# Forming the lower weight halves of some feed-forward units by an adding DMA

## The chip, the cores and the metric

One core of a Trainium2 chip runs the whole program. The metric is the time of one execution on the device in microseconds (us), the median over runs. Beside it stands the profile of one execution, taken by the hardware profiler: for each instruction its engine, its line in the kernel, its start and length, and what it waited for. TensorE appears as PE (matmuls) and PEld (loads of its stationary operand), VectorE as DVE, ScalarE as ACT, GpSimd as POOL, and SyncE, which issues most DMAs, as SP.

## What is computed

Two layers of an encoder trunk on a sequence of 256 positions with 1024 channels, in float32:

```python
for l in range(DEPTH):                       # DEPTH = 2
    h = swiglu(rmsnorm(x, ffn1_pre_g[l]), ffn1_w_in[l], ffn1_w_out[l])
    x = x + 0.5 * rmsnorm(h, ffn1_post_g[l])
    h = hybrid_mixer(rmsnorm(x, mix_pre_g[l]), ...)   # LRU, retention, short convolution
    x = x + rmsnorm(h, mix_post_g[l])
    h = swiglu(rmsnorm(x, ffn2_pre_g[l]), ffn2_w_in[l], ffn2_w_out[l])
    x = x + 0.5 * rmsnorm(h, ffn2_post_g[l])

def swiglu(u, w_in, w_out):                  # w_in 1024 x 5632, w_out 2816 x 1024
    gate, up = split(u @ w_in, 2)
    return (silu(gate) * up) @ w_out
```

There are four feed-forward stages (two in each layer) and two mixers. The change touches the feed-forward stages alone.

## The kernel before

**Weights as a stream of units.** All large weight matrices lie in HBM in the order in which they are used, cut into 568 units of 128 rows by 1024 columns (512 KB). Two neighbouring units make a pair, 1 MB, loaded by one DMA from SP's queue into a buffer named raw (line 88; three such buffers). TensorE multiplies in a reduced form of float32 (fp32r), so each unit is split in two: ACT rounds it to an upper part, tile whi (line 93), and DVE subtracts that from the raw weights to give a lower part, tile wlo (line 94). The activations are split likewise, and each product is three matmuls into the same accumulator (`mm3`, lines 272 to 275): upper activations by whi (L273), upper activations by wlo (L274), lower activations by whi (L275).

**How far the stream runs ahead.** There are eight buffers for whi and eight for wlo. `Stream.prep` forms the next unit. `Stream.fill` forms units until eight are alive, and `Stream.done` drops units that are used up and calls `fill`. A unit's buffer is that of the unit eight places before it, so its whi can be written only when TensorE has read the older one for the last time.

**A feed-forward stage** (`ffn`, line 307) has eleven steps s = 0 to 10, each of 256 hidden channels. A step takes four units of the input projection, `ui[s]`, and two of the output projection, `uo[s]`. In the stream they stand as ui[0], ui[1], uo[0], ui[2], uo[1], ui[3] and so on. In the middle of a stage (lines 365 to 375) one step runs like this on TensorE: `fin(s, 0)` and `fin(s, 1)` multiply the two blocks of 128 positions by the four units ui[s], 24 matmuls each; then `fout(s-1, 0)`, two transpositions of step s (`ftr`, line 334), `fout(s-1, 1)`, and two more transpositions. Each unit of ui[s] serves six matmuls in a row of a `fin`. ACT and DVE form silu(gate) times up (lines 325 and 326) behind each `fin`, and they split the transposed result (lines 258 and 259) behind each `ftr`.

**Order of the work.** The program's text gives each instruction a priority. A planner then lays the instructions on the engines, taking by priority what its own model of the machine holds ready, and each engine keeps that order on the chip. On each engine and each queue instructions start in order: one that waits holds back what stands behind it on the same engine.

**POOL in a feed-forward stage.** At the ends of stages POOL does two small operations of each normalisation (lines 201 and 202). In the first feed-forward stage it also computes constants of the mixer once, a chain of 24 small operations (`channel_consts`, lines 448 to 471, called through `mixer_consts` at step 4 in the text). Otherwise it does nothing there, and it issues no DMA anywhere in the kernel.

Of the kernel before, what the change touches and what calls it, by code (L numbers as in the profile page):

```python
# [11 lines left out]
F32 = mybir.dt.float32  # L12
# [3 lines left out]
ALU = mybir.AluOpType  # L16
# [12 lines left out]
UW = 1024  # L29
# [41 lines left out]
class Stream:  # L71


    def __init__(self, nc, wpool, w):
        self.nc, self.pool, self.w = nc, wpool, w
        self.n = 2 * w.shape[0]
        self.next = 0
        self.tiles = {}
        self.cur = 0

    def prep(self):
        nc, i = self.nc, self.next
        n = UW // 2 if i < FIRST else UW
        if i % 2 == 0:
            self.raw = self.pool.tile([P, 2 * UW], F32, tag="raw", name=f"raw{i}", bufs=RBUFS)
            m = n if i < FIRST else 2 * UW
            for k in range(0, 2 * UW, m):
                nc.sync.dma_start(self.raw[:, k:k + m], self.w[i // 2, :, k:k + m])
        raw = self.raw[:, (i % 2) * UW:(i % 2 + 1) * UW]
        hi = self.pool.tile([P, UW], F32R, tag="whi", name=f"whi{i}", bufs=WBUFS)  # L90
        lo = self.pool.tile([P, UW], F32R, tag="wlo", name=f"wlo{i}", bufs=WBUFS)
        for k in range(0, UW, n):
            nc.scalar.copy(hi[:, k:k + n], raw[:, k:k + n])  # L93
            nc.vector.tensor_sub(lo[:, k:k + n], raw[:, k:k + n], hi[:, k:k + n].bitcast(F32))  # L94
        self.tiles[i] = (hi, lo)
        self.next += 1

# [22 lines left out]
def trunk_kernel(ctx: ExitStack, tc: tile.TileContext, x_in, pos, gains, gain0, par, id_in, consts, gw, w, out):  # L120
    nc = tc.nc
# [16 lines left out]
    def tok():  # L138
        return tp.tile([P, 512], F32, tag="tok", name=nm("tok"), bufs=TOK)
# [4 lines left out]
    def spl(shape):  # L144
        return tp.tile(shape, F32R, tag="spl", name=nm("spl"), bufs=7)
# [7 lines left out]
    def ps_tr():  # L153
        return pp.tile([P, 512], F32, tag="tr", name=nm("pstr"), bufs=2)

    def ps_acc():
        return [pp.tile([P, 512], F32, tag="acc", name=nm("psacc"), bufs=4) for _ in range(2)]
# [31 lines left out]
    st = Stream(nc, wp, w)  # L189
# [66 lines left out]
    def split(h, lo, src, scale=None):  # L256
        if scale is None:
            act.copy(h, src)  # L258
            dve.tensor_sub(lo, src, h.bitcast(F32))  # L259
        else:  # L260
            act.mul(h, src, scale)
            dve.scalar_tensor_tensor(lo, src, scale, h.bitcast(F32), op0=ALU.mult, op1=ALU.subtract)

    def post(tb, acc, l, k, f, fast=False):
        r = rstd(acc, D, f, fast)
        t = halves(w4())
        for o, a, g in zip(t, acc, halves(gain_tiles[(l, k)])):
            dve.tensor_mul(o, a, g)
        for a, o in zip(t, halves(x[tb])):
            dve.scalar_tensor_tensor(o, a, r, o, op0=ALU.mult, op1=ALU.add)  # L270
# [6 lines left out]
    def inproj(us, tb, turn=None):  # L277

        ps = ps_in()
        for c in range(KD):  # L280
            if c == KD - 3 and turn is not None:
                turn()
            h, lo = st.get(us[c // 2])
            s = slice((c % 2) * 512, (c % 2 + 1) * 512)
            mm3(ps, uh[tb][:, c, :], ul[tb][:, c, :], h[:, s], lo[:, s], c == 0, c == KD - 1)
        return ps

    def inproj2(us):

        ps = [ps_in() for _ in range(NTB)]  # L290
        for k, u in enumerate(us):
            h, lo = st.get(u)
            for tb in range(NTB):
                for i in range(2):
                    c, s = 2 * k + i, slice(i * 512, (i + 1) * 512)
                    mm3(ps[tb], uh[tb][:, c, :], ul[tb][:, c, :], h[:, s], lo[:, s], c == 0, c == KD - 1)
        return ps

    def outproj(acc, blocks, us, first, last, ns=(0, 1)):

        for n in ns:
            for i, ((ah, al), u) in enumerate(zip(blocks, us)):
                h, lo = [halves(t)[n] for t in st.get(u)]
                mm3(acc[n], ah, al, h, lo, first and i == 0, last and i == len(us) - 1)


    def ffn(l, kpost, after, turn, during=None, start=False, fast=False):


        ui, uo, hT = {}, {}, {}  # L310
        for s in range(NS + 1):
            if s < NS:
                ui[s] = st.take(4)
            if s >= 1:
                uo[s - 1] = st.take(2)
        acc = [ps_acc() for _ in range(NTB)]

        def fin(s, tb, turn=None):
            gate_up(s, tb, [inproj(ui[s], tb, turn)])

        def gate_up(s, tb0, pss):
            for tb, ps in enumerate(pss, tb0):
                t = tok()
                with tc.high_priority(offset=CHAIN_LEAD if s == NS - 1 else 0):
                    act.activation(t[:, 0:256], ps[:, 0:256], AF.Silu, scale=fac[tb])  # L325
                    dve.scalar_tensor_tensor(t[:, 256:512], ps[:, 256:512], fac[tb], t[:, 0:256],  # L326
                                             op0=ALU.mult, op1=ALU.mult)
                hT[(s, tb)] = t

        def ftr(s, tb):  # L330
            t = hT[(s, tb)]
            pt = ps_tr()
            for i in range(2):
                pe.transpose(pt[:, i * P:(i + 1) * P], t[:, 256 + i * P:256 + (i + 1) * P], ident)  # L334
            hl = spl([P, 2, 256])
            with tc.high_priority(offset=CHAIN_LEAD if s == NS - 1 else 0):
                split(hl[:, 0, :], hl[:, 1, :], pt[:, 0:256])
            hT[(s, tb)] = hl

        def fout(s, tb, ns=(0, 1)):  # L340
            hl = hT[(s, tb)]
            outproj(acc[tb], [(hl[:, 0, c * P:(c + 1) * P], hl[:, 1, c * P:(c + 1) * P]) for c in range(2)],
                    uo[s], s == 0, s == NS - 1, ns)

        st.fill()
        if start:
            gate_up(0, 0, inproj2(ui[0]))
            st.done(ui[0])
            fin(1, 0)
            ftr(0, 0)  # L350
        else:
            fin(0, 0)
            fin(1, 0, turn)
            ftr(0, 0)
            fin(0, 1)
            st.done(ui[0])
        ftr(1, 0)
        fin(1, 1)
        ftr(0, 1)
        st.done(ui[1])  # L360
        fout(0, 0)
        fout(0, 1)
        ftr(1, 1)
        st.done(uo[0])
        for s in range(2, NS - 1):
            if s == 4 and during is not None:
                during()
            fin(s, 0)
            fin(s, 1)
            st.done(ui[s])  # L370
            fout(s - 1, 0)
            ftr(s, 0)
            fout(s - 1, 1)
            ftr(s, 1)
            st.done(uo[s - 1])
        e = NS - 1

        def tail(tb):
            fin(e, tb)
            fout(e - 1, tb, (0,))  # L380
            ftr(e, tb)
            fout(e - 1, tb, (1,))

        tail(0)
        fout(e, 0)
        with tc.high_priority(offset=CHAIN_LEAD):
            post(0, acc[0], l, kpost, 0.5)
            turn = after(0)
        tail(1)
        st.done(ui[e])  # L390
        st.done(uo[e - 1])
        fout(e, 1, (0,))
        if turn is not None:
            turn()
        fout(e, 1, (1,))
        st.done(uo[e])
        with tc.high_priority(offset=CHAIN_LEAD):
            post(1, acc[1], l, kpost, 0.5, fast)
            return after(1)
# [492 lines left out]
    for l in range(L):  # L892
        turn = ffn(l, G_F1POST, lambda tb: pre(tb, l, G_MPRE, False), turn,
                   mixer_consts if l == 0 else lambda: load_gain(l, G_MPRE), l == 0)
        load_gain(l, G_MPOST)
        load_gain(l, G_F2PRE)
        turn = mixer(l, lambda tb: pre(tb, l, G_F2PRE, True), turn)
        load_gain(l, G_F2POST)
        if l + 1 < L:
            load_gain(l + 1, G_F1PRE)  # L900
            turn = ffn(l, G_F2POST, lambda tb: pre(tb, l + 1, G_F1PRE, True), turn)
            load_gain(l + 1, G_F1POST)
        else:
            ffn(l, G_F2POST, store, turn, fast=True)
# [120 lines left out]
```

## Time and profile before

| | |
|---|---|
| median of 3 runs | 1677.73 us (1677.65 to 1677.97) |
| the profiled execution, its own time | 1678.78 us |
| its span, from the first to the last instruction | 1677.0 us |
| mean granted clock of TensorE | 0.997 of full speed |
| TensorE matmul busy | 1663.1 us (99% of the span) |
| DVE busy | 1069.0 us (64%) |
| ACT busy | 862.0 us (51%) |
| POOL busy | 78.6 us (5%) |
| read from HBM | 307.52 MB, 184 GB/s over the span |

Busy shares are averages over the whole span. Matmul records overlap their neighbours, so the length of one record is not its share of the time; the distance between the starts of two is. Idle time of an engine other than the one that sets the end costs nothing by itself. The launch and the end of a run lie outside the span: 1.78 us in the profiled execution.

### The profile page before, as it was taken

Reading aid. Unit: us, or ns where it says so; the run is one execution under the profiler, and the core shown is the slowest. Engines: PE = TensorE matmul, PEld = TensorE weight load, DVE = VectorE, ACT = ScalarE, POOL = GpSimd, SP = SyncE. Lnnn points to the kernel's source line nnn. Section 1 sums busy time; section 2 is a strip of 40 time slices with the busy share of each in tenths; the row PEclk is TensorE's granted clock in tenths of the full one; section 3 lists DMA queues with packets and bytes.
Section 4 is the critical chain, followed back from the end, with each engine's and each line's share of the span. In section 5 each row is a group of like instructions: output and inputs, shape, how many; then the busy total and the mean of one; then the engine's idle time right before and its main releaser. Section 6 shows DMA issues by size and latency. Waiting matters only on the chain.

```text
span 1677.0 us, 19458 instructions
## 1 busy us (share of the span) xinstructions
PE 1663.1 (99%) x7649; PEld 1372.3 (82%) x7649; DVE 1069.0 (64%) x1329; ACT 862.0 (51%) x1191; POOL 78.6 (5%) x110
## 2 busy tenths in 40 slices
PE   8999999999999999999999999999999999999998
PEld 7888788888888888888888887888888888888886
DVE  6655669956665657655565556799666566675553
ACT  6444567644544445544454445766445545464442
POOL 0300100000000002000000001000000000020000
PEclk9999999999999999999999999999999999999999
DMA  7555454555454444554465554545554454455451
GB/s 300 222 185 191 166 199 163 201 200 199 153 193 158 176 176 176 202 199 176 154 247 192 185 186 165 203 173 201 188 191 174 157 194 152 176 186 201 177 200 50
DMA packets 45163, 309.83 MB, mean 185 GB/s; under 512 B 5136, under 2 KB 5520, under 8 KB 8848
## 3 DMA queue, kind: packets, MB, share of 16 engines
q1 hardware_dynamic: 42768, 301.18, 49.2%
q10 hardware_dynamic: 2304, 7.41, 1.3%
q8 instruction: 60, 0.98, 0.2%
q14 instruction: 31, 0.25, 0.0%
HBM read 307.52 MB, written 1.05 MB: 184 GB/s over the span
## 4 chain that ended last, share of the span: by engine, by line
PE 97%; DVE 1%; issue 1%; POOL 0%; DMA 0%; ACT 0%; DVEq 0%; POOLq 0%; ACTq 0%
PE psin L273 21%; PE psin L274 21%; PE psin L275 21%; PE psacc L275 9%; PE psacc L273 9%; PE psacc L274 9%; PE pstr L334 1%; PE pstr L513 1%; DVE wlo L94 1%; PE pstr L237 1%; PE pstr L678 1%; PE pstr L750 0%; DMA g<-in_gain_dram 0%; PE pstr L274 0%; PE pstr L273 0%
## 5 line engine op out<-in xcount | busy, mean ns | idle before, releaser
L94 DVE TENSOR_TENSOR wlo<-raw,whi 128x1024 fp32r<-128x1024 f32 (+1 forms) x570 | 687.3, 1218 | 365.2 <-ACT whi L93 345.2
L93 ACT CAST whi<-raw 128x1024 fp32r<-128x1024 f32 (+1 forms) x570 | 591.6, 1049 | 295.0 <-PE psacc L275 148.3
L273 PE MATMUL psin<-whi,uh 128*128 128x512 f32 x1600 | 632.3, 395 | 2.8 <-ACT whi L93 2.3
L274 PE MATMUL psin<-wlo,uh 128*128 128x512 f32 x1600 | 626.1, 391 | 0.0
L275 PE MATMUL psin<-whi,ul 128*128 128x512 f32 x1600 | 624.7, 391 | 0.0
L273 PEld LDWEIGHTS psin<-whi,uh 128*128 128x128 f32 x1600 | 301.2, 188 | 62.9 <-ACT whi L93 2.5
L275 PEld LDWEIGHTS psin<-whi,ul 128*128 128x128 f32 x1600 | 300.9, 188 | 62.6
L274 PEld LDWEIGHTS psin<-wlo,uh 128*128 128x128 f32 x1600 | 301.2, 188 | 59.9 <-DVE wlo L94 0.6
L273 PE MATMUL psacc<-whi,spl 128*128 128x512 f32 x608 | 241.3, 397 | 0.0
L275 PE MATMUL psacc<-whi,spl 128*128 128x512 f32 x608 | 237.9, 391 | 0.7 <-DVE spl L259 0.7
L274 PE MATMUL psacc<-wlo,spl 128*128 128x512 f32 x608 | 237.2, 390 | 0.0
L275 PEld LDWEIGHTS psacc<-whi,spl 128*128 128x128 f32 x608 | 114.1, 188 | 25.5 <-DVE spl L259 1.5
L274 PEld LDWEIGHTS psacc<-wlo,spl 128*128 128x128 f32 x608 | 114.4, 188 | 22.2
L273 PEld LDWEIGHTS psacc<-whi,spl 128*128 128x128 f32 x608 | 114.2, 188 | 21.8
L325 ACT ACTIVATE tok<-psin,small 128x256 f32<-128x256 f32 x88 | 41.8, 475 | 173.2 <-PE psin L275 172.0
L326 DVE SCALAR_TENSOR_TENSOR tok<-psin,small,tok 128x256 f32<-128x256 f32 x88 | 42.3, 480 | 113.8 <-ACT tok L325 113.7
L201 POOL TENSOR_SCALAR small<-small 128x1 f32<-128x1 f32 x39 | 39.6, 1015 | 1545.0 <-ACT w L196 1544.3
L258 ACT CAST spl<-pstr 128x256 fp32r<-128x256 f32 (+1 forms) x104 | 41.1, 403 | 56.2 <-PE pstr L334 56.0
L259 DVE TENSOR_TENSOR spl<-pstr,spl 128x256 fp32r<-128x256 f32 (+1 forms) x104 | 47.3, 461 | 26.0 <-ACT spl L258 26.0
L501 ACT COPY tok<-psin 128x512 f32<-128x512 f32 x40 | 23.5, 587 | 62.7 <-PE psin L275 62.7
L258 ACT CAST spl<-w 128x1024 fp32r<-128x1024 f32 x16 | 16.6, 1051 | 40.7 <-DVE w L691 38.9
L334 PEld LDWEIGHTS pstr<-ident,tok 128*128 128x128 f32 x176 | 24.1, 139 | 15.1 <-DVE tok L326 4.0
(146 smaller groups left out, 957.6 us busy)
## 6 DMA issues: line engine op xcount, KB each, us to landing
raw<-in_w_dram SPq DMA_DIRECT2D x283, 1024.0 KB, 4.8
gain<-in_gains_dram ACTq DMA_DIRECT2D x10, 512.0 KB, 4.4
w<-in_gw_dram ACTq DMA_DIRECT2D x4, 512.0 KB, 3.5
x<-in_x_dram SPq DMA_DIRECT2D x2, 512.0 KB, 4.9
raw<-in_w_dram SPq DMA_DIRECT2D x4, 256.0 KB, 6.0
out_dram<-x SPq DMA_DIRECT2D x4, 256.0 KB, 2.0
ks<-in_consts_dram SPq DMA_DIRECT2D x1, 512.5 KB, 5.8
gain<-in_gains_dram SPq DMA_DIRECT2D x1, 512.0 KB, 5.7
```

The source lines that it names most:

```text
L93: nc.scalar.copy(hi[:, k:k + n], raw[:, k:k + n])
L94: nc.vector.tensor_sub(lo[:, k:k + n], raw[:, k:k + n], hi[:, k:k + n].bitcast(F32))
L201: first_e.tensor_scalar(r, ss[:, 0:1], more, EPS / (f * f), op0=ALU.add, op1=ALU.add)
L258: act.copy(h, src)
L259: dve.tensor_sub(lo, src, h.bitcast(F32))
L273: pe.matmul(ps, lhsT=xh, rhs=wh, start=first, stop=False)
L274: pe.matmul(ps, lhsT=xh, rhs=wl, start=False, stop=False)
L275: pe.matmul(ps, lhsT=xl, rhs=wh, start=False, stop=last)
L325: act.activation(t[:, 0:256], ps[:, 0:256], AF.Silu, scale=fac[tb])
L326: dve.scalar_tensor_tensor(t[:, 256:512], ps[:, 256:512], fac[tb], t[:, 0:256], op0=ALU.mult, op1=ALU.mult)
L334: pe.transpose(pt[:, i * P:(i + 1) * P], t[:, 256 + i * P:256 + (i + 1) * P], ident)
L501: act.copy(t, ps)
```

## The change

In each feed-forward stage the numbers of the second and fourth unit of every `ui[s]` are put into a set, in the first stage from s = 2 on. When `prep` comes to a unit of the set, it no longer subtracts on DVE. Instead ACT writes the raw weights times -1 into wlo, which rounds them to fp32r as the upper part was, so wlo holds the negated upper part. Then a DMA issued by POOL reads the same unit of the weights from HBM a second time and adds it onto wlo in place. The result is again the weights less their upper part. All other units keep the subtraction.

```diff
@@ class Stream
+        self.summed = set()
@@ prep
             nc.scalar.copy(hi[:, k:k + n], raw[:, k:k + n])
-            nc.vector.tensor_sub(lo[:, k:k + n], raw[:, k:k + n], hi[:, k:k + n].bitcast(F32))
+            if i in self.summed:
+
+                nc.scalar.mul(lo, raw, -1.0)
+                nc.gpsimd.dma_start(lo, self.w[i // 2, :, (i % 2) * UW:(i % 2 + 1) * UW],
+                                    accum_op=ALU.add)
+            else:
+                nc.vector.tensor_sub(lo[:, k:k + n], raw[:, k:k + n], hi[:, k:k + n].bitcast(F32))
@@ ffn
                 ui[s] = st.take(4)
+                if s > 1 or not start:
+                    st.summed.update(ui[s][1::2])
```

The set is filled when `ffn` is entered. A unit that was formed before that stays as it was.

## Rows read from the trace of the kernel before

**Rows 1.** The profile's first part: the span, then busy time, share and instruction count of each engine.

```profile
span 1677.0 us, 19458 instructions
PE 1663.1 (99%) x7649; PEld 1372.3 (82%) x7649; DVE 1069.0 (64%) x1329; ACT 862.0 (51%) x1191; POOL 78.6 (5%) x110
```

**Rows 2.** Waits of the matmul side of TensorE, all of them: who waited for whom, the sum in us, how often, the longest.

```profile
PE pstr L334 <- DVE tok L326: 2.7, 3, 1.2
PE psin L273 <- ACT whi L93: 2.3, 1, 2.3
PE pstr L187 <- DVE ones L184: 1.4, 1, 1.4
PE psacc L275 <- DVE spl L259: 0.7, 2, 0.3
PE psin L273 <- DVE tok L326: 0.5, 1, 0.5
```

**Rows 3.** Stretches of the span: start and end, length, then for each engine the busy time in the stretch with its instructions, the granted clock, the busy share of the DMA engines, and GB/s. The four stretches of 118 to 140 us lie in the middles of the four feed-forward stages; the last row is one step of the second stage.

```profile
42.00:176.00 134.00, 134.00 (x607) 110.42 (x606) 78.44 (x105) 61.67 (x83) 14.68 (x24) 1.00 0.54 197
...
700.00:818.00 118.00, 118.00 (x534) 97.20 (x533) 62.29 (x70) 53.88 (x70) 0.00 (x0) 1.00 0.52 188
...
870.00:1010.00 140.00, 140.00 (x633) 115.00 (x632) 73.85 (x83) 63.83 (x83) 0.00 (x0) 1.00 0.52 188
...
1530.00:1650.00 120.00, 120.00 (x544) 98.84 (x543) 63.50 (x72) 56.08 (x73) 0.00 (x0) 1.00 0.48 172
...
717.67:734.50 16.83, 16.83 (x80) 13.86 (x78) 8.90 (x10) 7.70 (x11) 0.00 (x0) 1.00 0.53 189
```

**Rows 4.** Groups of instructions over the whole span: line, engine, operation, output and input, count, then busy us and mean ns of one, then the engine's idle time before them and what ended it.

```profile
L94 DVE TENSOR_TENSOR wlo<-raw,whi 128x1024 fp32r<-128x1024 f32 (+1 forms) x570 | 687.3, 1218 | 365.2 <-ACT whi L93 345.2
...
L93 ACT CAST whi<-raw 128x1024 fp32r<-128x1024 f32 (+1 forms) x570 | 591.6, 1049 | 295.0 <-PE psacc L275 148.3 <-PE psin L275 108.9 <-issue 20.6
...
L326 DVE SCALAR_TENSOR_TENSOR tok<-psin,small,tok 128x256 f32<-128x256 f32 x88 | 42.3, 480 | 113.8 <-ACT tok L325 113.7
```

**Rows 5.** ACT in one step of the second feed-forward stage, in order of time: start, length, line, operation, and in brackets the idle time before it and what ended it. The casts of 724.78 and 726.14 form the third and fourth unit of the next step's input projection, those of 727.50 and 729.24 the two units of this step's output projection, and those of 733.88 and 735.09 the first two units of the input projection of the step after next.

```profile
724.78 1.05 ACT L93 CAST whi<-raw 128x1024 fp32r<-128x1024 f32 x1 [0.88 <-PE psin L275]
726.14 1.06 ACT L93 CAST whi<-raw 128x1024 fp32r<-128x1024 f32 x1 [0.30 <-PE psin L275]
727.50 1.06 ACT L93 CAST whi<-raw 128x1024 fp32r<-128x1024 f32 x1 [0.30 <-PE psin L275]
728.86 0.47 ACT L325 ACTIVATE tok<-psin,small 128x256 f32<-128x256 f32 x1 [0.30 <-PE psin L275]
...
735.09 1.05 ACT L93 CAST whi<-raw 128x1024 fp32r<-128x1024 f32 x1
```

**Rows 6.** Matmuls of TensorE that read those units, in the same columns: the transpositions behind `fout`, the first matmul of the next `fin`, the seventh pair of upper and lower in it (which is the first of the fourth unit), and in the step after it the first matmul and the first that reads the second unit's lower part.

```profile
734.36 0.38 PE L334 MATMUL pstr<-ident,tok 128*128 128x128 f32 x2
734.50 0.48 PE L273 MATMUL psin<-whi,uh 128*128 128x512 f32 x1
...
738.69 0.39 PE L273 MATMUL psin<-whi,uh 128*128 128x512 f32 x1
738.92 0.39 PE L274 MATMUL psin<-wlo,uh 128*128 128x512 f32 x1
...
751.32 0.48 PE L273 MATMUL psin<-whi,uh 128*128 128x512 f32 x1
...
753.02 0.39 PE L274 MATMUL psin<-wlo,uh 128*128 128x512 f32 x1
```

**Rows 7.** DMA issues over the span: destination and source, issuing queue, count, KB each, median us from issue to landing; and the shortest, median and longest landing of the weight loads.

```profile
raw<-in_w_dram SPq DMA_DIRECT2D x283, 1024.0 KB, 4.8
gain<-in_gains_dram ACTq DMA_DIRECT2D x10, 512.0 KB, 4.4
w<-in_gw_dram ACTq DMA_DIRECT2D x4, 512.0 KB, 3.5
...
DMA to landing us min/median/max: 4.7/4.8/8.8
```

**Rows 8.** SP's queue behind 728.4 in that step (the start of the first of three merged issues and the time to the last), and two stretches of the step in the columns of Rows 3.

```profile
728.48 9.52 SPq L88 DMA_DIRECT2D raw<-in_w_dram  x3
...
728.50:731.50 3.00, 3.00 (x16) 2.44 (x15) 2.81 (x3) 1.47 (x3) 0.00 (x0) 1.00 0.70 188
731.50:734.50 3.00, 3.00 (x18) 2.45 (x16) 0.46 (x2) 1.00 (x2) 0.00 (x0) 1.00 0.94 358
```

**Rows 9.** POOL in the first feed-forward stage, in order of time: the first operations of the chain of constants, its last, and the next operation behind it.

```profile
46.14 0.34 POOL L471 TENSOR_SCALAR hb<-pr 128x32 f32<-128x32 f32 x1 [32.84 <-DVE pr L886]
46.44 2.96 POOL L457 TENSOR_TENSOR cc<-base,cc 128x16 f32<-128x16 f32 x1
49.49 0.28 POOL L459 TENSOR_SCALAR cc<-cc 128x16 f32<-128x16 f32 x1
49.85 2.94 POOL L460 TENSOR_TENSOR cc<-cc,base 128x16 f32<-128x16 f32 x1
52.87 0.22 POOL L461 TENSOR_TENSOR cc<-cc,cc 128x16 f32<-128x16 f32 x1
...
62.47 0.22 POOL L470 TENSOR_TENSOR nsp<-nsp,cc 128x16 f32<-128x16 f32 x1
188.80 0.32 POOL L201 TENSOR_SCALAR small<-small 128x1 f32<-128x1 f32 x1 [126.11 <-ACT w L196]
```

**Rows 10.** The same stretch on ACT and TensorE: the casts of the second and the fourth unit of step 3, and the first matmul that reads the fourth unit's lower part.

```profile
42.53 1.05 ACT L93 CAST whi<-raw 128x1024 fp32r<-128x1024 f32 x1
...
50.46 1.05 ACT L93 CAST whi<-raw 128x1024 fp32r<-128x1024 f32 x1 [0.32 <-PE psin L275]
...
63.18 0.39 PE L274 MATMUL psin<-wlo,uh 128*128 128x512 f32 x1
```

## The prediction

> **What bounds the kernel now.** I read the engines' shares first: TensorE is busy for 1663.1 of 1677.0 us and no other engine for more than 64% [rows 1]. So a change can give time back only where TensorE stands idle, and can cost only where it makes TensorE wait. Next, TensorE's waits: all five groups together are 2.7 + 2.3 + 1.4 + 0.7 + 0.5 = 7.6 us, and not one of them waits for a lower weight part or for a load [rows 2]. Then the stretches. In the middles of all four feed-forward stages, where the change acts, TensorE is busy for the whole length, at the full granted clock [rows 3]. Last, one step in order of time, to see how early a lower part is ready before it is read [rows 5, 6].
>
> **How many units change.** A stage has eleven steps, but the stream has formed eight units of it before `ffn` fills the set: ui[0] and ui[1]. In the first stage those two steps are left out by the condition as well. So steps 2 to 10 count, with two units each: 9 x 2 = 18 a stage, 72 in all. I expect 72 DMAs from POOL.
>
> **What goes.** 72 subtractions on DVE of 1218 ns, 87.7 us [rows 4]. DVE is busy for 8.90 of the 16.83 us of a step [rows 3] and falls to about 6.5. TensorE has no wait for it in these stretches, so this is worth 0. The most it could be worth is the largest group that waits for DVE, 2.7 us [rows 2]; those sit where stages join, outside the stretches, and the units formed there are not in the set.
>
> **What comes on ACT.** 72 products over 128 x 1024 elements. The trace has no such product; the nearest row is the cast of the same shape with 1049 ns [rows 4], which I take, between 0.5 and twice that. In a step ACT goes from 7.70 to 7.70 + 2 x 1.05 = 9.8 us of 16.83 [rows 3], so it keeps over 40% idle. Queued behind the product of 727.20 are the cast of 727.50, now at 728.25, and the silu of 728.86, now at about 729.30 [rows 5]. The silu's 0.47 and DVE's 0.48 [rows 4] then end at about 730.3, and the transposition that needs them starts at 734.36 [rows 6]: 4 us of cover. Cost 0; with a product of twice the length, still 3 us of cover.
>
> **What comes on the DMA engines, and the wait that it adds.** This decides. TensorE's read of a lower part waited for DVE; now it waits for a DMA that POOL can issue only when ACT's product is done. Behind the waiting POOL instruction stand only the next such DMA and, in one place, the constants (below). Behind the waiting matmul stands everything.
>
> The time that is there, for the fourth unit: its cast starts at 726.14 and takes 1.06, the product 1.05, so the DMA may go at 728.25; the matmul that reads the sum starts at 738.92 [rows 5, 6]. That is 10.7 us. For the second unit: cast at 735.09, product done at 737.19, read at 753.02: 15.8 us. So the fourth unit is the tight one, 9 x 4 = 36 of them.
>
> The time that the DMA needs has no row, since no DMA here adds and none is issued by POOL. From below: a plain load of 512 KB lands in 3.5 us [rows 7]. From above: the longest weight load took 8.8 us [rows 7]; the sum must read 0.5 MB from HBM and 0.5 MB of wlo, 1 MB at the rate of a burst, and the rate of the stretch at share 0.94 is 358 GB/s, so 1.05 MB more are 2.9 us; if it is served last behind such a load it lands after 11.7 us. Between them I take the row of the same number of bytes, 4.8 us for 1 MB, and add the 2.9 us once, because the fourth unit's DMA goes out together with a pair: SP issues one at 728.48 and the DMA engines are then 0.70 and 0.94 busy for six us [rows 8]. That is 7.7 us, which leaves 10.7 - 7.7 = 3.0 us. The value is 0, and the upper end is (11.7 - 10.7) x 36 = 36 us.
>
> The Trainium skill (Collectives: The Full Stack, "Why ReduceScatter is half of AllGather") says that a reduction in the DMA engines goes at half the rate of a copy because it reads two sources, and not because of the adding. Had the DMA the cost of a plain load instead, it would land 1 to 4 us sooner; the sum stays 0 by either. No run here shows it yet.
>
> The pairs on SP's queue are hit as well: 2.9 us later each at worst. A pair issued at 728.48 is first cast one step later, at 724.78 + 16.83 = 741.61 [rows 5, 8], 13.1 us on, and needs 4.8. Cover 8 us, cost 0. A raw buffer is set free by the product's end (728.25) where it was the subtraction's (728.48 on SP), so nothing there gets later.
>
> **POOL's constants.** In the first stage POOL works without a pause from 46.14 to 62.69 on 24 operations [rows 9]. Step 3's second unit is cast at 42.53 and its product is done at 44.63, before that chain: free. Its fourth unit is cast at 50.46, the product is done at 52.56, in the midst of the chain, and TensorE reads the sum at 63.18 [rows 10]. Where the planner puts the DMA among the 24 isn't in the trace. At best it goes at 52.79, behind L460, and lands at 52.79 + 7.7 = 60.5: free. At worst it goes behind the last, at 62.69, lands at 70.4 and costs 7.2 us, once. It stands ahead of the constants in the program's text and so is taken as soon as the planner holds its product done; I take a place near the best and a cost of 0. From 55.5 on, each microsecond later costs one. POOL's next operation is at 188.80, so nobody else waits behind it.
>
> **Sum.** 0 for DVE, 0 for ACT, 0 for the DMAs, 0 for the constants. The profiled execution took 1678.78, its span 1677.0 and 1.78 around it; the median lies 1.05 under it. Against its own time I forecast 1678.8, and as a median 1677.7. A measurement of this kernel tells some 0.2% from no change, 3.4 us.
>
> **Rivals.**
>
> 1. *The sum lands too late (slower).* The place is the L274 matmul of each step's fourth unit; the point is a landing over 10.7 us behind ACT's product; the price is 36 times the excess, since each step's lead starts anew from TensorE's own release of the buffer. At the upper end above, 36 us: 1714. An excess of 0.1 us is already 3.6 us. For it: the DMA is issued into the busiest six us of the step, and its issue on POOL has no row. Against it: the DMA engines are about half busy over a step (0.53), and even the longest load (8.8) would be in time. Chance 0.20.
>
> 2. *The constants delay one sum (slower).* 1677.7 + 7.2 = 1685 at worst, over the bound of 3.4 us when the DMA goes later than about 58.9. For it: POOL is full for 16.5 us over just this time. Against it: the order of the text. Chance 0.14.
>
> 3. *DVE's relief reaches TensorE (faster).* 1677.7 - 2.7 = 1675.0 at most, if the waits of L334 for DVE vanish [rows 2]. Against it: they lie where no unit changes. And 2.7 us is under 0.2%. Chance of more than that, with all else unforeseen, 0.03.
>
> 4. *It does not do what it says.* If the set came too late for all units, no DMA on POOL would be seen and the time would be 1677.7 as well; the count tells, not the time. Chance 0.01; it counts as no change.
>
> **How the numbers follow.** My forecast, all covered, has 0.62. With rival 4 that is 0.63 within 0.2%. Slower: 0.20 + 0.14 = 0.34. Faster: 0.03. The likeliest case's own range is 1676.5 to 1681. For 8 in 10 it must hold rival 2 and the small excesses of rival 1, up to 0.35 us a step (12 us): 1676.5 to 1690. What lies above is the larger part of rival 1, some 0.15, and little below.
>
> **What would show it.** 72 DMAs issued by POOL and 72 products on ACT of about 1.05 us; L94 falls from 570 to 498. TensorE's waits keep their five groups, with none of L274 for a DMA; the four stretches stay full. The landing behind POOL's issue should be 5 to 9 us, and the pairs' median a little over 4.8. Rival 1 would show as 36 waits of about equal length, rival 2 as one wait near 63 us. I am wrong if the sums land over 10.7 us behind their products, or if TensorE's matmuls go further apart while these DMAs run.

## The result and the profile after

The changed kernel takes 1688.53 us (median of 4 runs, 1687.73 to 1690.65), the kernel before 1677.69 us beside it (4 runs, 1677.43 to 1677.97). The ratio is 1.0067, with an interval of 1.0049 to 1.0084: 10.8 us slower. The profiled execution took 1690.65 us with a span of 1688.9, so its span is 11.9 us longer than that of before [rows 1].

In the changed kernel the lines stand some rows lower: the cast is L94, the new product on ACT L97, the new DMA L98, the subtraction L101, and the three matmuls of a product L280 to L282. First the busy time of the engines, from the profile's first part.

```profile
PE 1665.6 (99%) x7649; PEld 1373.0 (81%) x7649; DVE 981.9 (58%) x1257; ACT 925.4 (55%) x1263; POOL 139.1 (8%) x182
```

Then the groups of the lines that the change touches, in the columns of [rows 4].

```profile
L101 DVE TENSOR_TENSOR wlo<-raw,whi 128x1024 fp32r<-128x1024 f32 (+1 forms) x498 | 599.4, 1216 | 413.9 <-ACT whi L94 405.8
...
L98 POOL DMA_DIRECT2D wlo<-in_w_dram x72 | 62.6, 874 | 536.2 <-ACT wlo L97 353.2
L97 ACT ACTIVATE wlo<-raw 128x1024 fp32r<-128x1024 f32 x72 | 76.4, 1061 | 3.1 <-PE psin L281 0.7
```

And the DMA issues, in the columns of [rows 7].

```profile
raw<-in_w_dram SPq DMA_DIRECT2D x283, 1024.0 KB, 5.2
wlo<-in_w_dram POOLq DMA_DIRECT2D x72, 512.0 KB, 8.1
```

The change did what it says: 72 subtractions fewer, 72 products of 1061 ns and 72 DMAs more, and each of these lands 8.1 us (median) behind POOL's issue. DVE lost 87.1 us of work. Now the waits of TensorE's matmul side, all that the view lists, as in [rows 2].

```profile
PE psin L281 <- DMA wlo<-in_w_dram: 8.3, 1, 8.3
PE pstr L343 <- DVE tok L335: 2.5, 3, 1.1
PE psin L280 <- ACT whi L94: 2.3, 1, 2.3
PE pstr L194 <- DVE ones L191: 1.4, 1, 1.4
PE psin L280 <- DVE tok L335: 1.1, 1, 1.1
PE psacc L282 <- DVE spl L266: 0.7, 2, 0.3
```

The old groups stand almost as they were. One line is new, and its count is 1: of 72 sums a single one held TensorE up for long, by 8.3 us. (Two others came some 0.2 us late, too little for this view; they follow in the part on why the prediction was wrong.) The stretches of [rows 3], and the same 16.83 us of the second stage, say where it is.

```profile
42.00:176.00 134.00, 125.68 (x555) 102.90 (x554) 54.08 (x83) 68.96 (x89) 26.08 (x39) 0.96 0.83 241
700.00:818.00 118.00, 118.00 (x535) 97.19 (x534) 45.10 (x56) 66.41 (x84) 12.07 (x14) 1.00 0.89 254
870.00:1010.00 140.00, 140.00 (x633) 114.98 (x632) 55.51 (x69) 81.24 (x104) 14.71 (x17) 1.00 0.89 258
1530.00:1650.00 120.00, 120.00 (x543) 98.85 (x542) 45.59 (x57) 67.07 (x86) 12.07 (x14) 1.00 0.89 255
...
717.67:734.50 16.83, 16.83 (x78) 13.86 (x77) 6.45 (x8) 9.49 (x13) 1.73 (x2) 1.00 0.88 245
```

The three later stages are full at the full clock, as before. Only the first lost time, and its granted clock is 0.96. The DMA engines' share rose to 0.89 there (0.48 to 0.52 before), so in the second stage by 71% where the bytes rose by 35%, from 188 to 254 GB/s [rows 3], and TensorE's busy time fills all three.

The wait itself is found on three engines. ACT finished the product of step 3's fourth unit at 50.64:

```profile
49.58 1.06 ACT L97 ACTIVATE wlo<-raw 128x1024 fp32r<-128x1024 f32 x1
```

POOL, in order of time as in [rows 9], was then in the second operation of the chain of constants and took the DMA only behind the last of it:

```profile
48.33 0.34 POOL L480 TENSOR_SCALAR hb<-pr 128x32 f32<-128x32 f32 x1 [3.23 <-DVE pr L895]
48.64 2.93 POOL L466 TENSOR_TENSOR cc<-base,cc 128x16 f32<-128x16 f32 x1
...
62.98 0.22 POOL L479 TENSOR_TENSOR nsp<-nsp,cc 128x16 f32<-128x16 f32 x1
63.46 1.87 POOL L98 DMA_DIRECT2D wlo<-in_w_dram  x2 [0.26 <-issue]
```

And TensorE (one row per matmul, as in [rows 6]) started its last matmul before the wait at 62.35 and the next at 71.06:

```profile
62.35 0.39 PE L280 MATMUL psin<-whi,uh 128*128 128x512 f32 x1
71.06 0.80 PE L281 MATMUL psin<-wlo,uh 128*128 128x512 f32 x1 [8.32 <-DMA wlo<-in_w_dram]
71.66 0.63 PE L282 MATMUL psin<-whi,ul 128*128 128x512 f32 x1
72.08 0.63 PE L280 MATMUL psin<-whi,uh 128*128 128x512 f32 x1
...
77.20 0.44 PE L280 MATMUL psin<-whi,uh 128*128 128x512 f32 x1
77.48 0.40 PE L281 MATMUL psin<-wlo,uh 128*128 128x512 f32 x1
```

The distances of the starts tell a second loss. At the full clock two matmuls start some 0.227 us apart; behind the wait they start 0.427 us apart, until 77.2. Three stretches just there, in the columns of [rows 3], show the granted clock:

```profile
62.00:71.00 9.00, 0.74 (x4) 0.28 (x2) 0.00 (x0) 0.00 (x0) 2.81 (x6) 0.78 0.94 226
71.00:77.40 6.40, 6.34 (x15) 4.99 (x16) 0.60 (x2) 1.52 (x2) 0.00 (x0) 0.51 0.04 8
77.40:90.00 12.60, 12.60 (x59) 10.33 (x58) 10.10 (x21) 7.96 (x10) 1.46 (x2) 1.00 0.66 208
```

The clock fell to the lower of its two levels (0.51, that is 1.2 instead of 2.4 GHz) while TensorE stood idle, and stayed there for the first 6.4 us of the work that followed. The bill, from the starts of the matmuls: 71.06 - 62.35 - 0.23 = 8.5 us of standing still; then 15 distances that took 77.48 - 71.06 = 6.42 us where 15 x 0.227 = 3.41 do at the full clock, 3.0 us. Together 11.5 of the 11.9 us that the span grew.

### The profile page after: what moved, and what is told of

The parts are those of the page before. It is cut to its first block, busy times and chain, and to the rows that moved or that the text cites. A ratio compares the mean times of both kernels' runs of the same rounds, so it can differ in the third digit from the quotient of the medians.

```text
span 1688.9 us, 19714 instructions
## 1 busy us (share of the span) xinstructions
PE 1665.6 (99%) x7649; PEld 1373.0 (81%) x7649; DVE 981.9 (58%) x1257; ACT 925.4 (55%) x1263; POOL 139.1 (8%) x182
## 3 DMA queue, kind: packets, MB, share of 16 engines
q0 software_dynamic: 10368, 37.75, 12.8%
## 4 chain that ended last, share of the span: by engine, by line
PE 94%; DVE 2%; DMA 1%; POOL 1%; issue 1%; ACT 0%; DVEq 0%; SPq 0%; POOLq 0%; ACTq 0%
PE psin L281 21%; PE psin L280 21%; PE psin L282 21%; PE psacc L282 9%; PE psacc L280 9%; PE psacc L281 9%; DVE wlo L101 1%; PE pstr L343 1%; PE pstr L522 1%; PE pstr L244 1%; PE pstr L687 1%; DMA chan<-in_par_dram 0%; DMA wlo<-in_w_dram 0%; PE pstr L759 0%; DMA g<-in_gain_dram 0%
## 5 line engine op out<-in xcount | busy, mean ns | idle before, releaser
L101 DVE TENSOR_TENSOR wlo<-raw,whi 128x1024 fp32r<-128x1024 f32 (+1 forms) x498 | 599.4, 1216 | 413.9 <-ACT whi L94 405.8
L94 ACT CAST whi<-raw 128x1024 fp32r<-128x1024 f32 (+1 forms) x570 | 587.0, 1047 | 274.9 <-PE psacc L282 146.0
L280 PE MATMUL psin<-whi,uh 128*128 128x512 f32 x1600 | 632.4, 395 | 3.4 <-ACT whi L94 2.3
L281 PE MATMUL psin<-wlo,uh 128*128 128x512 f32 x1600 | 627.4, 392 | 8.4 <-DMA wlo<-in_w_dram 8.3
L282 PE MATMUL psin<-whi,ul 128*128 128x512 f32 x1600 | 625.7, 391 | 0.0
L281 PEld LDWEIGHTS psin<-wlo,uh 128*128 128x128 f32 x1600 | 301.6, 189 | 69.7 <-DMA wlo<-in_w_dram 9.6
L280 PEld LDWEIGHTS psin<-whi,uh 128*128 128x128 f32 x1600 | 301.4, 188 | 63.9 <-ACT whi L94 2.5
L282 PEld LDWEIGHTS psin<-whi,ul 128*128 128x128 f32 x1600 | 301.4, 188 | 62.5
L280 PE MATMUL psacc<-whi,spl 128*128 128x512 f32 x608 | 241.1, 397 | 0.0
L282 PE MATMUL psacc<-whi,spl 128*128 128x512 f32 x608 | 237.9, 391 | 0.7 <-DVE spl L266 0.7
L281 PE MATMUL psacc<-wlo,spl 128*128 128x512 f32 x608 | 237.2, 390 | 0.0
L282 PEld LDWEIGHTS psacc<-whi,spl 128*128 128x128 f32 x608 | 114.1, 188 | 25.4 <-DVE spl L266 1.5
L281 PEld LDWEIGHTS psacc<-wlo,spl 128*128 128x128 f32 x608 | 114.4, 188 | 22.2
L280 PEld LDWEIGHTS psacc<-whi,spl 128*128 128x128 f32 x608 | 114.2, 188 | 21.8
L98 POOL DMA_DIRECT2D wlo<-in_w_dram x72 | 62.6, 874 | 536.2 <-ACT wlo L97 353.2
L97 ACT ACTIVATE wlo<-raw 128x1024 fp32r<-128x1024 f32 x72 | 76.4, 1061 | 3.1 <-PE psin L281 0.7
```

The lines of the kernel that those rows point to most:

```text
L97: nc.scalar.mul(lo, raw, -1.0)
L98: nc.gpsimd.dma_start(lo, self.w[i // 2, :, (i % 2) * UW:(i % 2 + 1) * UW], accum_op=ALU.add)
L280: pe.matmul(ps, lhsT=xh, rhs=wh, start=first, stop=False)
L281: pe.matmul(ps, lhsT=xh, rhs=wl, start=False, stop=False)
L282: pe.matmul(ps, lhsT=xl, rhs=wh, start=False, stop=last)
```

## The experiments

Theory A: the whole loss is that one DMA in POOL's queue behind the constants, and the clock that falls in the wait. Theory B: the traffic of all 72 DMAs, or their late landing, costs time everywhere.

**All but that one unit.**

```diff
                 if s > 1 or not start:
                     st.summed.update(ui[s][1::2])
+                if s == 3 and start:
+                    st.summed.discard(ui[s][3])
```

> The change with one of its 72 units taken out: the fourth unit of step 3 of the first feed-forward stage is subtracted on DVE as before. Theory A (POOL's queue: that one adding DMA stands behind the 24 operations of the constants, and TensorE's wait for it, with the slower clock behind that wait, is the whole loss): no wait of L281 for a DMA, 1677.5 to 1678.5 us, ratio to before within 0.1%. Theory B (the loss comes from the traffic of 72 adding DMAs, spread over the stages): 71 of 72 stay, so about 10.7 of the 10.8 us stay, 1688 us.

Measured: 1678.83 us (10 runs, 1678.11 to 1680.44; before 1677.69 in 19 runs), ratio 1.0007, interval 0.9998 to 1.0017. TensorE has no wait for a DMA at all, and the first stage is full again:

```profile
42.00:176.00 134.00, 134.00 (x605) 110.06 (x604) 59.77 (x90) 74.54 (x96) 27.13 (x39) 1.00 0.89 256
```

With the same DMA share of 0.89 and 71 of 72 sums, 9.7 of the 10.8 us are gone. Theory B falls for them.

**That one unit alone.**

```diff
-                if s > 1 or not start:
-                    st.summed.update(ui[s][1::2])
+                if s == 3 and start:
+                    st.summed.add(ui[s][3])
```

> Only that one unit is formed by the adding DMA, the other 71 are subtracted on DVE. Theory A: the constants end near 62.7 us as before, the DMA behind them meets less traffic and lands 6 to 8 us later, at 69 to 71, where TensorE wants it at 63.2; one wait of 5.5 to 8 us and some 2 to 3 us of slower clock behind it: 1684.5 to 1688.5 us. Theory B: one DMA of 0.5 MB costs nothing that can be measured: 1677.7 us.

Measured: 1687.76 us (4 runs, 1686.63 to 1689.44), ratio 1.0061, interval 1.0046 to 1.0076. The waits again show one single line for a DMA:

```profile
PE psin L281 <- DMA wlo<-in_w_dram: 7.0, 1, 7.0
```

One DMA of 512 KB costs 10.1 us of 1677.69. The other 71 left 1.1 us in the experiment above, which its interval does not tell from nothing.

**All 72, the constants ordered behind the first stage's DMAs.** `channel_consts()` leaves `mixer_consts` and is called behind the loop over steps, with an order that holds for POOL:

```diff
+        if start:
+            with tc.issue_after(st.sent.ins):     # the last adding DMA issued so far
+                channel_consts()
@@ mixer_consts
-        channel_consts()
```

> All 72 units by the adding DMA, and the constants ordered on POOL behind the first stage's last adding DMA (near 160 us; the next work of POOL is at 188.8 and the constants take 16.5 us). Nothing is left out. Theory A: TensorE never waits for an adding DMA, 1677.3 to 1678.5 us, though the DMA engines stay 0.89 busy in the stages. Theory B: traffic and units are unchanged, so 1688 us.

Measured: 1678.82 us (10 runs, 1678.08 to 1680.13), ratio 1.0007, interval 0.9997 to 1.0017. On POOL the DMA now goes at 51.19 instead of 63.46, and TensorE waits for a DMA only once, for 0.2 us (step 2 of the last stage):

```profile
51.19 0.86 POOL L98 DMA_DIRECT2D wlo<-in_w_dram  x1 [5.83 <-DVE wlo L101]
```

So neither the change nor that unit is dear by itself; the place of its DMA in POOL's queue is.

**The constants behind the loop in the text alone**, with the same move but without the order. This tries the reason that the prediction gave for the place.

```diff
+        if start:
+            channel_consts()
@@ mixer_consts
-        channel_consts()
```

> All 72 units, and the constants moved in the program's text alone: their call stands behind the loop over the steps, after all adding DMAs of the stage, with no order given. Theory A with the planner as I now take it (it puts operations where its model holds them ready, and these have all they need once the parameters are loaded): POOL's order stays as in the changed kernel, one wait of 8 to 9 us near 62 us, 1687 to 1691 us. If the text's order decides, as the prediction had it: the constants go last, no wait, 1678 us.

Measured: 1688.93 us (1 run). The chain still runs ahead of the DMA, which goes at 64.77; first TensorE's wait, then POOL:

```profile
PE psin L281 <- DMA wlo<-in_w_dram: 7.4, 1, 7.4
```

```profile
64.29 0.22 POOL L481 TENSOR_TENSOR nsp<-nsp,cc 128x16 f32<-128x16 f32 x1
64.77 1.86 POOL L98 DMA_DIRECT2D wlo<-in_w_dram  x2 [0.26 <-issue]
```

Both places in the text give the same order on POOL. What makes the planner choose it was not tried further; an explicit order undoes it.

**How much for how long a delay.** The chain is cut in two; its head stays where it was, and the rest is ordered behind the DMA of step 3's fourth unit alone. In the first run the head ends with the first of the seven polynomial steps, in the second with the fifth.

```diff
@@ channel_consts
-        for d in (13, 11, 9, 7, 5, 3, 1):
+        for d in (13,):                            # second run: (13, 11, 9, 7, 5)
...
@@ ffn, behind the loop over steps
+        if start:
+            with tc.issue_after(st.sent[ui[3][3]].ins):
+                rest()                             # the other operations of the chain
```

> All 72 units by the adding DMA. The chain of constants is cut in two: its first 9 operations (to the first of the seven polynomial steps) stay where they were, the other 15 are ordered behind the DMA of step 3's fourth unit. In the trace of the changed kernel the first part would end at 57.4 us, so the DMA goes then, lands 7.6 us later at about 65.0, and the matmul that could start at about 62.8 waits some 2.2 us. Theory A (each us that POOL holds the DMA back past 55 costs one, and the clock falls only behind a long idle): wait 2.2 us, granted clock near 1.0 behind it, 1678.8 + 2.2 = 1681.0 us. Rival A2 (any wait there brings the clock down to its lower level): wait 2.2 and 3 us for the clock behind it, 1684.0 us.

> As the run before, cut four polynomial steps later: the first 17 operations stay, 7 are ordered behind the DMA. The first part would end at 61.0 us, the DMA lands at about 68.6, the matmul waits some 5.8 us. Theory A: 1678.8 + 5.8 = 1684.6 us if the clock stays, 1687.6 if it falls as it did behind the wait of 8.3 us. The two runs with the changed kernel give three points of wait against clock.

Measured: 1685.77 us (5 runs, 1683.35 to 1687.62; before 1678.26 in 9 runs), ratio 1.0042, interval 1.0029 to 1.0056; and 1687.56 us (4 runs, 1687.13 to 1688.34), ratio 1.0056, interval 1.0042 to 1.0070. In both traces the wait is longer than expected. In the first (the matmuls are L281 to L283 here, the DMA L99), the clock in three stretches:

```profile
62.00:67.20 5.20, 0.79 (x4) 0.33 (x2) 0.00 (x0) 0.00 (x0) 2.55 (x8) 0.99 0.99 302
67.20:70.50 3.30, 3.23 (x8) 2.55 (x9) 0.18 (x1) 0.47 (x1) 0.00 (x0) 0.50 0.88 170
70.50:90.00 19.50, 19.50 (x89) 16.03 (x88) 13.73 (x30) 11.55 (x16) 1.71 (x2) 1.00 0.70 201
```

then POOL's issue of the DMA:

```profile
57.51 0.96 POOL L99 DMA_DIRECT2D wlo<-in_w_dram  x1 [0.21 <-issue]
```

and TensorE's matmul that waited for it:

```profile
67.28 0.79 PE L282 MATMUL psin<-wlo,uh 128*128 128x512 f32 x1 [4.49 <-DMA wlo<-in_w_dram]
```

The DMA went at 57.51, as worked out, but the matmul went on 9.8 us later and not 7.6, in a stretch in which the DMA engines had a share of 0.99. So the wait was 4.5 us and not 2.2. And the clock fell here too, for a shorter time (0.50 from 67.2 to 70.5). Of the two, A2 is nearer: each of these waits, from 4.5 us up, brought the clock down. The wait of 2.2 us, at which the two would have parted, did not come about; the run with all units has shorter ones. From the starts of the matmuls, in us, worked out as for the changed kernel:

| run | DMA goes | matmul goes on | standing still | half clock | sum | median less before |
|---|---|---|---|---|---|---|
| constants behind | 51.19 | in time | 0 | 0 | 0 | 1.1 |
| short head | 57.51 | 67.28 | 4.7 | 1.6 | 6.3 | 7.5 |
| long head | 60.85 | 69.79 | 7.2 | 2.1 | 9.3 | 9.3 |
| that one unit | 64.00 | 71.31 | 7.1 | 2.3 | 9.4 | 10.1 |
| moved in the text | 64.77 | 70.51 | 7.6 | 1.7 | 9.3 | 11.2 (1 run) |
| the change | 63.46 | 71.06 | 8.5 | 3.0 | 11.5 | 10.8 |

The sums come from one execution each, the last column from medians; the two go together within 1.3 us, but for the single run moved in the text (1.9). What the clock adds does not follow the length of the wait alone: behind 7.6 us of standing still it is less than behind 7.1.

**All four units of each step**, 144 DMAs, the constants behind them as above: `st.summed.update(ui[s])` in place of `ui[s][1::2]`. This looks for the limit of the lead.

> All four units of each ui[s] by the adding DMA, 144 instead of 72, the constants ordered behind the first stage's DMAs. Theory A (72 are hidden only because the DMA engines have room left): their busy share in a step's 16.83 us went from 0.53 to 0.89, so 72 more ask for 0.53 + 2 x 0.36 = 1.25; the DMA engines become the bound, a step takes some 21 us, and 36 steps cost about 36 x 4.2 = 150 us: about 1830 us, with waits of the first matmul of lower parts in every step. Rival (the share counts time in which an engine merely holds a packet, and there is room left): no waits for the DMA, 1679 us.

Measured: 1747.12 us (2 runs, 1745.71 to 1748.54), ratio 1.0410, interval 1.0391 to 1.0429. The group of waits, and the second stage:

```profile
PE psin L281 <- DMA wlo<-in_w_dram: 42.3, 27, 3.3
```

```profile
700.00:818.00 118.00, 109.05 (x471) 87.34 (x470) 26.89 (x38) 68.77 (x86) 20.92 (x25) 0.96 1.03 291
```

The DMA engines are full (1.03), the sums land 9.9 us (median) behind POOL's issue, and 27 of them come too late. So what the prediction called rival 1 is real; with 72 sums it is barely reached. The size was off: 69 us instead of 150. I had added up shares to 1.25 of a step, 21 us; measured, a step takes 18.7 us (mean of the 36, from the starts of the matmuls), with the full engines moving 291 GB/s. So the shares do not simply add; why was not tried. Of the 69 us, 42.3 are these waits. The mean granted clock of the run is 0.985 where it was 0.997, which by an estimate from these two is some 21 us more of 1746.7.

This run also has waits shorter than those of the table. Behind one of 2.6 us the clock fell too, and was at its lower level from 976.2 to 979.6:

```profile
975.14 0.50 PE L281 MATMUL psin<-wlo,uh 128*128 128x512 f32 x1 [2.57 <-DMA wlo<-in_w_dram]
```

```profile
976.20:979.60 3.40, 3.40 (x10) 2.62 (x9) 0.48 (x1) 1.14 (x2) 0.00 (x0) 0.50 1.03 322
```

Behind one of 1.35 us, at 770.39, the granted clock of the next 3.6 us is 1.00.

**A plain copy in the place of the sum**, the constants behind: the same DMA without `accum_op`.

> As the run with the constants behind, but POOL's 72 DMAs copy the weights into wlo and add nothing; the lower part of those units is therefore the raw weights. Same instructions, same waits, same bytes from HBM; only the reading of wlo and the adding go. If the reading of the second source is what makes the DMA dear: landing falls from 8.1 us to 4 or 5, the DMA share in the stretches from 0.89 to about 0.71 (0.53 and a third of it more for a third more bytes). If POOL's issue is what makes it dear: landing stays at 8 us and the share at 0.89. The time is 1678 to 1679 us by both.

Measured: 1681.16 us (1 run), no wait for such a DMA. The group of the DMAs on POOL, then their landing among the DMA issues, then the second stage:

```profile
L98 POOL DMA_DIRECT2D wlo<-in_w_dram x72 | 38.7, 538 | 565.4 <-ACT wlo L97 355.3
```

```profile
wlo<-in_w_dram POOLq DMA_DIRECT2D x72, 512.0 KB, 5.7
```

```profile
700.00:818.00 118.00, 118.00 (x535) 97.19 (x534) 45.13 (x56) 66.45 (x84) 7.39 (x14) 1.00 0.70 251
```

At the same bytes moved (251 and 254 GB/s) the copies add 0.70 - 0.52 = 0.18 to the DMA engines' share, the sums 0.89 - 0.52 = 0.37: twice as much. By the time that their own packets took, the factor is smaller. These are the rows of POOL's queue (packets, MB, share of the 16 engines' span), first for the changed kernel and then for the copies:

```profile
q0 software_dynamic: 10368, 37.75, 12.8%
```

```profile
q0 software_dynamic: 10368, 37.75, 7.9%
```

That is 1.6 times as much, for as many packets and bytes; the rest of the factor of two lies in the other queues' packets, which took longer beside the sums than beside the copies. The copies also land in 5.7 us instead of 8.1, and POOL is busy for 538 ns with each instead of 874. So a sum is dearer than a copy, on the DMA engines and on POOL; whether by the reading of the second source or by the adding itself, this run can't tell, since it leaves out both. The Trainium skill (Collectives: The Full Stack, "Why ReduceScatter is half of AllGather"), which the prediction weighed, says of a collective's reduction that it goes at half the rate because it reads two sources; here the factor lies between 1.6 and 2.

The single time lies 2.9 us above before's median, and not in the work of the stages: DVE's last operations start at 1672.64 in this trace and at 1672.52 in that of before, and 1.42 us later no engine computes any more. First this kernel, then the kernel before:

```profile
1672.64 1.42 DVE L276 SCALAR_TENSOR_TENSOR x<-w,small,x 128x512 f32<-128x512 f32 x2
```

```profile
1672.52 1.42 DVE L270 SCALAR_TENSOR_TENSOR x<-w,small,x 128x512 f32<-128x512 f32 x2
```

The spans end at 1679.4 and 1677.0: 5.3 and 3.0 us behind that work, in which the last rows are stored and the program is closed. It is one execution; what held its end up stays open.

**What stays open.** With the late sum gone, both medians still stand 1.1 us over before's. Their intervals include a ratio of 1, and in their profiled executions the spans are 1676.9 and 1677.4 us against 1677.0. The traces show where part of it can lie. In all kernels with an adding DMA the profiled span ends 3.6 to 3.8 us behind DVE's last operation, in that of before 3.0. The work itself ends no later in these two than before; with the constants behind, DVE's last operations start here:

```profile
1672.24 1.42 DVE L277 SCALAR_TENSOR_TENSOR x<-w,small,x 128x512 f32<-128x512 f32 x2
```

So some 0.6 to 0.8 us come once, at the program's end, even with a single such DMA (3.6). For the remaining tenths I can't tell whether the 71 or 72 DMAs cost anything in the stages.

## Why the prediction was wrong

The time was forecast as 1677.7 us and is 1688.5: inside the range of 1676.5 to 1690, but by rival 2, which had 0.14. The steps in their order:

**The bound, the count, DVE and ACT were right.** TensorE is still busy for 99%; 72 units changed. DVE fell to 6.45 us in the step (6.5 forecast) and this was worth nothing: the waits for DVE's `tok` were 2.7 + 0.5 us and are 2.5 + 1.1. (All groups that wait for DVE were 5.3 us and not the 2.7 that the prediction took as the most; none of it came.) ACT rose to 9.49 us (9.8), its product takes 1061 ns (1049), and no matmul waits for it.

**The lead of the sums was right in the middle of the stages and too long at their start.** I took 7.7 us for the landing, between 3.5 and 11.7; the median is 8.1. In the middle the fourth unit's product ends 11.9 us before the matmul that reads the sum (737.80 and 749.73 in one step; I had 10.7), and the latest of these sums landed 2.1 us ahead. But I had read the lead off one step in the middle and taken it for all 36. The fourth unit of step 2 has 10.5 us in the three later stages (688.74 and 699.25 in the second), and there the sums landed 9.9, 10.3 and 10.4 us behind POOL's issue, which itself goes 0.3 us behind the product. The last two came too late by 0.2 us each. In the last stage the pair of matmuls starts 0.42 us apart and not 0.227:

```profile
1528.79 0.39 PE L280 MATMUL psin<-whi,uh 128*128 128x512 f32 x1
1529.21 0.50 PE L281 MATMUL psin<-wlo,uh 128*128 128x512 f32 x1
```

So the value of 0 held within 0.4 us, but with no room left at these places, and with the traffic doubled it no longer holds (the run with all units). The pairs land 0.4 us later (5.2), for which 2.9 were allowed.

**The step that failed is POOL's constants:** "It stands ahead of the constants in the program's text and so is taken as soon as the planner holds its product done; I take a place near the best and a cost of 0." The DMA stood behind the whole chain, 12.8 us after its product was done. I had the two ends right, 0 and 7.2 us, and chose between them by a rule on the text that no row bore out. The premise was true, for the DMA does stand ahead of the chain in the text, but it did not decide: the chain went first, and went first again in the run with its call moved further behind. Why the planner chose so stays open. With no row for the place, the cost was as open as the range between its ends, and 0.14 was too little.

**Its size was off as well**, by two terms. The worst end was 7.2 us, and 8.5 were lost. The chain started at 48.33 and not at 46.14 [rows 9], for its parameters took 8.25 us to land where they had taken 5.6; in the run with a single sum they took 5.5, so this goes with the new traffic. The chain itself ran faster, in 14.9 us instead of 16.5, and the DMA went at 63.46 instead of 62.69. In the chain of waits of the changed kernel:

```profile
39.70 8.25 DMA chan<-in_par_dram
...
63.46 7.56 DMA wlo<-in_w_dram
71.06 0.80 PE psin L281
```

The matmul went on at 71.06 instead of 70.4, and TensorE was ready for the sum at about 62.6 and not at 63.18 [rows 10]. And the sum had no term for the clock: the wait was priced as the time of standing still, where another 3.0 us followed it at the lower level.

**The rivals.** Rival 1 came with 72 sums only as 0.2 us at two places, at another step than the one it was reckoned from, and comes with 144. Rival 2 came, at its worst end and dearer. Rival 3 brought nothing. Rival 4 is excluded by the counts.

## What to carry to other kernels

An instruction that is issued from an idle engine's queue is only as early as what the planner puts ahead of it on that queue: look for any block of other work that the engine does in that time, even once, and give the order explicitly instead of inferring it from the text. When TensorE is the bound, price a wait of a few microseconds above its own length (one of 2.6 us was enough here), for the matmuls behind it ran at half clock for a while. A DMA that adds took 1.6 to 2 times the DMA engines' time of one that copies the same bytes; count with that before the engines are full. Read a lead off the first steps of a stage too, and not off one in the middle.

## What the runs showed of the hardware that was not expected

- TensorE's clock fell with single waits of 2.6 to 8.3 us in the midst of work at full rate, and the work behind them first ran at the lower level (granted 0.50 and 0.51): for 3.3 us behind the wait of 4.5, for 6.4 us behind that of 8.3, though for only 3.5 us behind that of 7.4. Behind the waits of 4.5 us and more it cost 1.6 to 3.0 us on top. The Trainium skill (TensorE: Matmul & The Clock Gate, "Part 1: The HAM clock gate (the "warmup" mystery)") says that the clock is gated by a monitor of how busy TensorE is; these rows agree.
- POOL is busy with the issue of one adding DMA for 874 ns, and with that of a plain one for 538 ns, at the same 512 KB. The prediction had named this issue as something without a row.
- The DMA engines' share of 0.89 over whole stages cost TensorE no measurable time beyond two waits of 0.2 us, though the landing of single sums spread from 5.3 to 10.4 us.
